# The order of the first transfers, and 1/rms behind the first products of the last FFN

## The chip, the cores and the metric

The kernel runs on one core of one Trainium2 chip. The metric is the device time of one execution in microseconds; the kernel before has a median of 1949.0 us in three runs (1946.32 to 1955.2). The engines are TensorE (PE, its weight loads are listed as PEld), VectorE (DVE), ScalarE (ACT), GpSimd (POOL) and SyncE (SP), which here issues the transfers.

## The reference

A backbone of two layers works on 256 latent and 256 context tokens of width 1024, all in fp32. Each layer has a SwiGLU FFN of width 2816, a mixer (eight attention heads, four gated DeltaNet heads, one output projection) and a second FFN. In front of each stands an RMS norm with a shift and a scale that come from a condition vector through `w_mod`:

```
y = xf * lax.rsqrt(jnp.mean(xf * xf, axis=-1, keepdims=True) + RMS_EPS)
h = modulate(rms_norm(x, gain), shift, scale)      # h * (1 + scale) + shift
gate, up = jnp.split(h @ w_in, 2, axis=-1)
x = x + 0.5 * gate_mod * ((jax.nn.silu(gate) * up) @ w_out)
```

The mods are `silu(c) @ w_mod[l] + b_mod[l]`, nine vectors of 1024 for the latent tokens and nine for the context. In the second layer the output projection and the last FFN are made for the latent tokens alone.

## The kernel before, in words

**Layout.** x lies transposed: eight tiles `x[d]` of 128 features by 512 tokens, the latent half in columns 0 to 255. A feature here means such a tile. fp32 operands are split in a high and a low part (`hh`, `hl` for the modulated x, `wh`, `wl` for weights: a cast on ACT, then a subtraction on DVE), and `mm3` makes each product as three matmuls: high by high, high by low, low by high. The times below count these matmuls as products.

**An FFN.** A unit is 128 columns of gate and 128 of up; it takes 8 features x 2 x 3 = 48 products and two PSUM tiles, each 512 tokens wide in the first three FFNs and 256 wide in the last (`ns == 1`). There are 22 units, in groups of 8, 8, 2 and 4; the out-product of a group follows a group later. The first two units of an FFN are begun as soon as the first half of the tokens is normed. In the very first FFN it is three units, taken feature by feature (L1111), with weights that come in half tiles (`weight_part`).

**A norm** has four steps: squares of x as soon as a feature is added up (`square_sum`), column sums of these on PE with a matrix of ones (`norm_stats`), the spread of 1/rms over the partitions, again on PE (`norm_spread`), and for each feature a product with gain, scale and 1/rms on DVE, the shift on ACT and the low part on DVE (`norm_apply`).

**The start.** The first two mods are made on PE from 32 transfers of `w_mod` (tiles `n`, 256 KB each), in products with 32 columns (`sc` is silu of c). The copies and transpositions behind them give `md`, and with it the features. Later mods are made on DVE, as sums of products over `w_mod` rows (tiles `junk`, 512 KB for two of them), laid in as filler.

**The order.** Nothing is issued in program order. `Build` records all work as nodes; `plan()` lays them out seven times with a list scheduler, for each engine, with the durations of `cost_of`, the delays of a table `LAT` between engines and a priority, and picks the order and the buffers; this is then written out engine by engine. In gaps of PE that the planner foresees to be longer than `WARM[1]` it puts matmuls on zeros (`zero`, L672), which nothing reads. All other instructions are written at one line of the emitter, L680 in the profile of before (L681 afterwards).

**Around the change.** `main` and `program` (L1864 to L1937) hold the start: the calls of `load` and `features` in L1907 to L1918, which the planner is free to move. `next_norm` makes the function `after` that starts the norm behind a residual addition; the last output projection calls it once for the latent half.

## Time and profile before

| | |
|---|---|
| median of three runs | 1949.0 us |
| profiled execution | 1952.2 us, span 1950.4 us |
| granted clock of TensorE, mean of the span | 0.991 |
| PE busy | 1901.5 us, 97% |
| DVE busy | 1366.0 us, 70% |
| ACT busy | 833.3 us, 43% |
| transfers | 280.96 MB, 144 GB/s in the mean |

The profiled execution is one of its own and stands 3.2 us above the median. PE is the engine that sets the time; its gaps and its clock are the places to look at. A row of the timeline gives the start, the busy time, engine, line, operation, what is written and read (buffer numbers left out), the count of like instructions in it, and in brackets how long the engine was idle before and what ended that.

### The profile page before, as it was taken

To read this page: it belongs to the slowest core of one execution; us is meant where nothing else is said; L and a number is where in the kernel's file an instruction comes from. 1 tells how busy PE (TensorE), PEld (TensorE's weight loads), DVE (VectorE), ACT (ScalarE), POOL (GpSimd) and SP (SyncE) were. 2 spreads that over 40 slices of the span, in tenths; PEclk is the share of its full clock that TensorE was granted. 3 is DMA by queue.
4 is the path that set the end of the run, shared out by engine and by line. 5 is a ranking of instruction groups with operands and counts; after the bars stand their busy time and mean duration, and the time that the engine had idled before them with its cause. 6 is when DMAs were issued, how large, how long until landed. Compare 5 with 4: busy or idle time off the path is not lost.

```text
span 1950.4 us, 29083 instructions
## 1 busy us (share of the span) xinstructions
PE 1901.5 (97%) x11145; PEld 1617.4 (83%) x11145; DVE 1366.0 (70%) x2776; ACT 833.3 (43%) x1612; POOL 26.9 (1%) x31
## 2 busy tenths in 40 slices
PE   8999999999999999999999999999999989899999
PEld 5888887787886879888888898888889877689999
DVE  5666677799987978666653586556337988986555
ACT  5322221258838455222222342221125974755433
POOL 1000000000001000000000000000000000000000
PEclk9999999999998999999999999999999999999999
DMA  9555555553324213555553245656334243136654
GB/s 329 179 153 160 162 177 175 170 169 117 112 81 117 98 44 95 165 162 179 166 162 102 72 146 179 201 177 203 110 98 147 88 114 109 44 114 201 184 182 122
DMA packets 104474, 280.96 MB, mean 144 GB/s; under 512 B 27024, under 2 KB 30480, under 8 KB 104336
## 3 DMA queue, kind: packets, MB, share of 16 engines
q1 hardware_dynamic: 104336, 279.12, 45.9%
q8 instruction: 87, 1.43, 0.3%
q14 instruction: 51, 0.42, 0.1%
HBM read 270.69 MB, written 8.39 MB: 143 GB/s over the span
## 4 chain that ended last, share of the span: by engine, by line
PE 76%; DVE 13%; ACT 4%; DMA 4%; issue 2%; SPq 0%; DVEq 0%; ACTq 0%
PE ps L680 76%; DVE d L680 3%; DVE n L680 2%; DMA wr<-w_mod 2%; DVE wl L680 2%; ACT d L680 1%; DVE wh L680 1%; ACT n L680 1%; DVE junk L680 1%; ACT wh L680 1%; DVE t L680 1%; DVE s L680 1%; DVE x L680 1%; ACT s L680 1%; ACT L680 1%
## 5 line engine op out<-in xcount | busy, mean ns | idle before, releaser
L680 PE MATMUL ps<-s,wh 128*128 128x512 f32 (+1 forms) x3344 | 912.9, 361 | 1.0 <-DVE s L680 0.5
L680 PEld LDWEIGHTS ps<-s,wh 128*128 128x128 f32 x3344 | 592.8, 189 | 100.3 <-issue 1.4
L680 PE MATMUL ps<-s,wl 128*128 128x512 f32 (+1 forms) x1672 | 603.5, 361 | 0.9 <-DVE wl L680 0.9
L680 ACT CAST wh<-wr 128x1024 fp32r<-128x1024 f32 (+2 forms) x341 | 350.4, 1037 | 479.1 <-PE ps L680 328.6
L680 DVE TENSOR_TENSOR wl<-wr,wh 128x1024 fp32r<-128x1024 f32 (+2 forms) x341 | 408.3, 1208 | 97.1 <-ACT wh L680 93.6
L680 DVE CUSTOM_DVE_ANT_0 junk<-wr,m,sm 128x1024 bf16<-128x1024 f32 x224 | 287.6, 1284 | 235.0 <-DMA wr<-w_mod 231.9
L680 PEld LDWEIGHTS ps<-s,wl 128*128 128x128 f32 x1672 | 314.8, 188 | 48.6 <-DVE wl L680 1.6
L680 PE MATMUL ps<-d,wh 128*128 128x256 f32 (+1 forms) x1344 | 300.4, 319 | 6.9 <-DVE x L680 3.9
L680 PEld LDWEIGHTS ps<-d,wh 128*128 128x128 f32 x1344 | 223.1, 191 | 30.3 <-issue 9.3
L680 PE MATMUL ps<-d,wl 128*128 128x256 f32 (+1 forms) x672 | 212.8, 317 | 1.2 <-DVE wl L680 1.2
L680 PE MATMUL ps<-n,wh 128*128 128x512 f32 (+1 forms) x640 | 178.3, 365 | 0.0
L680 DVE SCALAR_TENSOR_TENSOR x<-ps,hg,x 128x256 f32<-128x256 f32 x224 | 97.4, 478 | 93.2 <-PE ps L680 93.1
L680 ACT ACTIVATE d<-ps 128x512 f32<-128x512 f32 (+2 forms) x108 | 56.9, 529 | 237.1 <-PE ps L680 236.7
L680 PE MATMUL ps<-wh,s 128*128 128x512 f32 (+1 forms) x544 | 154.2, 360 | 0.3 <-DVE s L680 0.3
L680 PEld LDWEIGHTS ps<-d,wl 128*128 128x128 f32 x672 | 128.3, 191 | 9.5 <-DVE wl L680 1.7
L680 PEld LDWEIGHTS ps<-n,wh 128*128 128x128 f32 x640 | 115.4, 189 | 20.8
L680 PE MATMUL ps<-n,wl 128*128 128x512 f32 (+2 forms) x416 | 130.6, 347 | 0.7 <-DVE n L680 0.7
L680 DVE TENSOR_TENSOR d<-d,d 128x256 f32<-128x256 f32 (+29 forms) x310 | 111.6, 381 | 16.6 <-ACT d L680 12.0
L680 PEld LDWEIGHTS ps<-wh,s 128*128 128x128 f32 x544 | 96.4, 188 | 19.5 <-issue 5.2
L680 PE MATMUL ps<-wl,s 128*128 128x512 f32 (+1 forms) x272 | 96.6, 355 | 0.6 <-DVE wl L680 0.6
L680 DVE TENSOR_TENSOR d<-d,ps 128x512 f32<-128x512 f32 (+1 forms) x88 | 54.4, 618 | 58.4 <-PE ps L680 40.6
L680 PEld LDWEIGHTS ps<-n,wl 128*128 128x128 f32 x416 | 71.9, 189 | 10.7 <-issue 0.8
(163 smaller groups left out, 1563.7 us busy)
## 6 DMA issues: line engine op xcount, KB each, us to landing
wr<-w_in SPq DMA_DIRECT2D x171, 512.0 KB, 4.3
wr<-w_mod SPq DMA_DIRECT2D x128, 512.0 KB, 4.0
wr<-w_out SPq DMA_DIRECT2D x104, 512.0 KB, 4.2
wr<-wd SPq DMA_DIRECT2D x24, 512.0 KB, 3.8
n<-w_mod SPq DMA_DIRECT2D x32, 256.0 KB, 5.5
wr<-wg SPq DMA_DIRECT2D x8, 528.0 KB, 3.6
xd<-x SPq DMA_DIRECT2D x16, 256.0 KB, 4.5
x<-xd SPq DMA_DIRECT2D x16, 256.0 KB, 3.6
```

The source lines that it names most:

```text
L680: getattr(eng, name)(*[rv(x) for x in a], **{q: rv(x) for q, x in k.items()})
```

## The change

It has four parts.

1. The first transfers. While `nc.settled` is true, nodes of SP get a priority by their number, so SP issues them in program order. The program's order is changed with it: the mods of a feature come behind the weights' half tiles of that quarter or ahead of them, as the diff shows.
2. The planner's numbers: the delay behind a transfer, the bytes per microsecond, the thresholds for zero products, and a few durations. The whole order is made anew with them.
3. 64 columns of the constants that nothing reads are left out.
4. The last FFN. `norm_raw` writes, feature by feature, x times gain and scale in two parts without 1/rms, and the shift as two more columns; the first two units' products run on these 258 columns (`ffn_mm_raw`). `ffn_act_raw` multiplies gate and up by 1/rms (`self.rms`) and adds the shift's column when the sums are there. The other 20 units use the normed features as before.

```diff
+        n.settled = self.settled and eng == "sync"
...
-    "sync": {"tensor": 2.1, "vector": 2.1, "scalar": 2.1, "gpsimd": 2.1, "sync": 2.1},
+    "sync": {"tensor": 2.8, "vector": 2.8, "scalar": 2.8, "gpsimd": 2.8, "sync": 2.1},
...
-WARM = (0.8, 0.6, 0.7)
+WARM = (0.8, 0.3, 0.85)
...
+        self.prio = [n.i - 1e6 if n.settled else p for p, n in zip(self.prio, rec.nodes)]
...
-        return max(0.48, byts / 359e3) if eng == "sync" else 1.04
+        return max(0.48, byts / 330e3) if eng == "sync" else 1.04
...
+        if name == "tensor_tensor_reduce":
+            return 0.19 + n / 960
...
+    def norm_raw(self, lc, m, d):
...
+        nc, O, F32, a = self.nc, self.O, self.F32, self.na[:, d, 0:1]
+        x, c, e = self.x[d][:, :TL], slice(TL, T), slice(T, T + 2)
+        hh, hl, sh = self.hh[d], self.hl[d], lc["md"][:, 8 * m + d, 0:1].to_broadcast([128, 2])
+        nc.scalar.activation(hh[:, c], x, self.A.Copy, scale=a)
+        nc.vector.scalar_tensor_tensor(hl[:, c], x, a, hh[:, c].bitcast(F32), O.mult, O.subtract)
+        nc.vector.tensor_copy(hh[:, e], sh)
+        nc.vector.tensor_tensor(hl[:, e], sh, hh[:, e].bitcast(F32), O.subtract)
...
+            if raw:
+                self.rms = self.slot("rms")[:, :TL]
+                self.nc.scalar.copy(self.rms, bs[:, :TL])
...
+    def ffn_mm_raw(self, u):
+        w, p = u
+        for k in range(KD):
+            for i in range(2):
+                r = slice((k % 4 * 2 + i) * 128, (k % 4 * 2 + i + 1) * 128)
+                self.mm3(p[i][:, :TL + 2], (w[k // 4][0][:, r], w[k // 4][1][:, r]), (self.hh[k][:, TL:], self.hl[k][:, TL:]), k == 0, k == KD - 1)
+
+    def ffn_act_raw(self, u, tag):
...
+        nc.vector.tensor_tensor(g[:, c], pg[:, c], self.rms, O.mult)
+        nc.vector.tensor_copy(b[:, 0:1], pg[:, TL:TL + 1])
+        nc.scalar.activation(g[:, c], g[:, c], self.A.Silu, bias=b[:, 0:1])
+        nc.vector.tensor_tensor(t[:, c], pu[:, c], self.rms, O.mult)
+        nc.vector.tensor_copy(b[:, 1:2], pu[:, TL:TL + 1])
+        nc.vector.scalar_tensor_tensor(g[:, c], t[:, c], b[:, 1:2], g[:, c], O.add, O.mult)
...
                 with nc.urgent(100):
                     self.add_x(d, ps, gate, (s,))
                     self.square_sum(d, s)
+                    if after.raw:
+                        after.raw(d)
...
+        nc.settled = True
         self.cond()
...
-        load(0, 0)
         features(0, 0, 1)
-        load(0, 1, 2)
+        load(0, 0, 1, 2)
         features(0, 1, 1)
+        features(1, 0, 2)
         load(1, 0, 1, 2)
-        features(1, 0, 2)
+        features(2, 0, 2)
         for f in range(2):
             u[f].append(self.weight_begin())
         load(2, 0, 1)
-        features(2, 0, 2)
+        features(3, 0, 2)
         load(3, 0, 1)
-        features(3, 0, 2)
+        self.nc.settled = False
```

On PE at the start, these rows of before stand behind the last product of `w_mod`; `s` are features, `wh` and `wl` the halves of a unit's weights, `ps` its PSUM tiles:

```order
L680 MATMUL ps_485<-s_491,wh_449 128x512
L680 MATMUL ps_485<-s_506,wh_449 128x512
L680 MATMUL ps_485<-s_491,wl_475 128x512
L680 MATMUL ps_502<-s_491,wh_449 128x512
L680 MATMUL ps_502<-s_506,wh_449 128x512
L680 MATMUL ps_502<-s_491,wl_475 128x512
```

In the new order products of `w_mod` (32 columns, from tiles `n`) stand between the FFN's in this way from the first FFN product on:

```order
L681 MATMUL ps_397<-s_442,wh_303 128x512
L681 MATMUL ps_397<-s_449,wh_303 128x512
L681 MATMUL ps_397<-s_442,wl_379 128x512
L681 MATMUL ps_411<-n_424,sc_79 32x128 x4
L681 MATMUL ps_418<-s_442,wh_303 128x512
L681 MATMUL ps_418<-s_449,wh_303 128x512
L681 MATMUL ps_418<-s_442,wl_379 128x512
L681 MATMUL ps_411<-n_438,sc_79 32x128 x4
```

Before has 18 FFN products ahead of the last product of `w_mod`, the new order has 75.

On PE at the last norm, before has zero products around the column sums of the squares (`con` by `d`) and the spread of 1/rms (`d` by `con`):

```order
L672 LDWEIGHTS zero_83
L672 MATMUL ps_15895<-zero_83 128x256
L680 MATMUL ps_15918<-con_188,d_15792 128x1 x2
L672 LDWEIGHTS zero_83
L672 MATMUL ps_15921<-zero_83 128x256
```

Now the products on the raw x follow the last ones of the output projection (`d` by `wh`) at once:

```order
L681 MATMUL ps_15950<-s_15556,wh_15802 128x258
L681 MATMUL ps_15950<-s_15564,wh_15802 128x258
L681 MATMUL ps_15950<-s_15556,wl_15832 128x258
L681 MATMUL ps_15926<-d_15699,wh_15775 128x256
L681 MATMUL ps_15926<-d_15717,wh_15775 128x256
L681 MATMUL ps_15926<-d_15699,wl_15797 128x256
L681 MATMUL ps_15962<-s_15556,wh_15802 128x258
L681 MATMUL ps_15962<-s_15564,wh_15802 128x258
L681 MATMUL ps_15962<-s_15556,wl_15832 128x258
L681 MATMUL ps_15950<-s_15580,wh_15802 128x258
```

The column sums stand 24 products behind the last one of the projection, and there are no zero products any more. Three raw products have moved ahead of it.

On DVE at the norm behind the first FFN of layer 0, before has a reduction over a tile of `w_mod` (`junk`) just ahead of the last unit's product of gate and up and the additions to x:

```order
L680 TENSOR_TENSOR wl_2874<-wr_2773,wh_2869 128x1024
L680 TENSOR_TENSOR d_2898<-d_2898,ps_2832 128x512
L680 ISA junk_803,md_400<-wr_2887,m_638,sm_370 128x1024
L680 ISA md_400 128x1
L680 TENSOR_TENSOR d_2920<-d_2898,d_2912 128x512
L680 TENSOR_TENSOR wl_2922<-wr_2807,wh_2905 128x1024
L680 SCALAR_TENSOR_TENSOR x_79<-ps_2900,hg_1226,x_79 128x256
```

Now both reductions of such a tile stand ahead of the product of gate and up:

```order
L681 TENSOR_TENSOR wl_2882<-wr_2783,wh_2877 128x1024
L681 ISA junk_910,md_326<-wr_2866,m_724,sm_85 128x1024
L681 ISA md_326 128x1
L681 ISA junk_910,md_326<-wr_2866,m_761,sm_85 128x1024
L681 ISA md_326 128x1
L681 TENSOR_TENSOR d_2906<-d_2906,ps_2841 128x512
L681 TENSOR_TENSOR wl_2923<-wr_2817,wh_2915 128x1024
L681 TENSOR_TENSOR d_2931<-d_2906,d_2921 128x512
L681 SCALAR_TENSOR_TENSOR x_170<-ps_2908,hg_1316,x_170 128x256
```

One more reduction has moved ahead of the additions to x.

## Rows read from the trace of the kernel before

**Rows 1.** Page, busy us of an engine, its share of the span.
```profile
PE 1901.5 (97%) x11145; PEld 1617.4 (83%) x11145; DVE 1366.0 (70%) x2776; ACT 833.3 (43%) x1612; POOL 26.9 (1%) x31
```
**Rows 2.** Windows, FFN products of the start: us, busy (count), clock, DMA share, GB/s.
```profile
0.00:50.00 50.00, 17.45 (x65) 0.93 0.96 330
0.00:100.00 100.00, 67.45 (x281) 0.97 0.74 249
```
**Rows 3.** Timeline of PE at the start.
```profile
28.80 0.80 PE L680 MATMUL ps<-s,wh 128*128 128x512 f32 x1
...
30.48 0.73 PE L680 MATMUL ps<-s,wh 128*128 128x512 f32 x2
...
31.74 0.74 PE L680 MATMUL ps<-s,wh 128*128 128x512 f32 x2
...
34.11 1.30 PE L680 MATMUL ps<-n,sc 128*32 128x128 f32 x40
...
38.69 0.42 PE L680 MATMUL ps<-n,sc 128*32 128x128 f32 x8
```
**Rows 4.** Timeline of PE at the last norm.
```profile
1750.61 0.28 PE L680 MATMUL ps<-d,wl 128*128 128x256 f32 x1
1750.73 1.38 PE L672 MATMUL ps<-zero 128*128 128x256 bf16 x11
1752.46 0.61 PE L680 MATMUL ps<-con,d 128*128 128x1 f32 x4 [0.36 <-DVE d L680]
...
1754.19 0.70 PE L680 MATMUL ps<-d,con 128*128 128x256 f32 x2 [0.23 <-DVE d L680]
...
1756.64 0.39 PE L680 MATMUL ps<-s,wh 128*128 128x256 f32 x1 [0.26 <-DVE s L680]
```
**Rows 5.** Timeline of PE at the norm behind the first FFN.
```profile
385.30 0.77 PE L680 MATMUL ps<-d,wh 128*128 128x256 f32 x2 [3.86 <-DVE x L680]
...
404.04 0.61 PE L680 MATMUL ps<-con,d 128*128 128x1 f32 x4 [4.05 <-DVE d L680]
```
**Rows 6.** Windows of PE, PEld, DVE, ACT, POOL; then clock, DMA share, GB/s.
```profile
25.00:30.00 5.00, 4.42 (x42) 2.37 (x42) 4.33 (x14) 2.54 (x6) 0.00 (x0) 0.66 0.99 342
385.00:390.00 5.00, 4.70 (x29) 4.73 (x30) 5.00 (x12) 0.00 (x0) 0.00 (x0) 0.69 0.44 129
600.00:650.00 50.00, 46.28 (x383) 36.04 (x381) 35.67 (x98) 36.56 (x113) 6.44 (x5) 0.90 0.41 133
1550.00:1600.00 50.00, 44.40 (x221) 36.53 (x222) 45.66 (x132) 39.90 (x102) 3.53 (x2) 0.93 0.28 80
```
**Rows 7.** Chain of waits, its last link: start, us, what.
```profile
1760.53 186.06 PE ps L680 x1556
```
**Rows 8.** Timeline of ACT and DVE at the start.
```profile
12.83 1.28 ACT L680 ACT_TABLE_LOAD   x1
...
16.64 0.37 ACT L680 COPY d<-ps 128x256 f32<-128x256 f32 x1 [0.25 <-PE ps L680]
...
23.51 1.23 DVE L680 SCALAR_TENSOR_TENSOR d<-x,na,d 128x256 f32<-128x256 f32 x3
...
24.66 0.88 DVE L680 SCALAR_TENSOR_TENSOR s<-d,md,s 128x256 fp32r<-128x256 f32 x2
...
26.21 0.62 ACT L680 CAST wh<-wr 128x512 fp32r<-128x512 f32 x1 [0.91 <-DMA wr<-w_in]
```
**Rows 9.** DMA issues: count, KB each, median us to landing.
```profile
n<-w_mod SPq DMA_DIRECT2D x32, 256.0 KB, 5.5
```
**Rows 10.** Timeline of ACT and DVE at the last norm.
```profile
1749.71 0.40 ACT L680 ACTIVATE d<-x 128x256 f32<-128x256 f32 x1
...
1754.92 1.26 DVE L680 SCALAR_TENSOR_TENSOR d<-x,na,ps 128x256 f32<-128x256 f32 x3 [0.79 <-PE ps L680]
```
**Rows 11.** Timeline of DVE at the norm behind the first FFN.
```profile
380.94 1.28 DVE L680 CUSTOM_DVE_ANT_0 junk<-wr,m,sm 128x1024 bf16<-128x1024 f32 x1 [3.96 <-DMA wr<-w_mod]
...
383.89 3.22 DVE L680 SCALAR_TENSOR_TENSOR x<-ps,hg,x 128x256 f32<-128x256 f32 x8
```

## The prediction
> **What bounds the kernel now.** I read the page's busy shares first. TensorE is busy 1901.5 us [rows 1] of a span of 1950.4, so only about 49 us can be won by closing its gaps, and everything else only by taking products away or by a higher granted clock. The change takes away no product of the reference. So I looked for gaps of PE, in the windows of the whole span and then in the PE timeline, in each place that the change touches. There are four kinds. The start: the first FFN product stands at 28.80, and 65 products are done at 50 us [rows 2, 3]. The last norm: between the last output-projection product and the stream of the last FFN [rows 4]. The norm behind the first FFN, where PE waits twice [rows 5]. And stalls inside the mixers [rows 6]. The last link of the chain of waits is 186 us of PE without a break [rows 7]: behind 1760.53 nothing can be won but by an earlier start of it, and every microsecond closed ahead of it is a microsecond of the end.

> **Part 1, the first transfers in program order.** Before, nearly all first modulation products come ahead of the FFN: 18 FFN products (six groups of three) stand before the last of them at 38.69 [rows 3]. Afterwards 75 do, in 25 groups of three, and between them stand 24 sets of four w_mod products (the trace counts 8 for such a set). Two numbers make the term: when the first group starts, and what a period costs.

> The start. Feature 0 now needs only four w_mod tiles, and the half tiles of the weights are requested behind them. So the scale by 1/rms sets it. Its copies end at 17.0 before (16.64 + 0.37 [rows 8]). ACT has three weight casts of 0.62 around these copies, but one pair of table loads of 1.28 fewer ahead [rows 8]; I take 17.4. From the first scaled feature to its low part the rows run from 23.51 to 24.66 + 0.44 (half of the two in that row), 1.6 us [rows 8]; the modulation's small sums ahead of it I estimate at 0.6. So the first product starts at 17.4 + 0.6 + 1.6 = 19.6, 9.2 earlier than 28.80.

> The period. In the one stretch of before in which the two kinds alternate at full speed, a group starts at 30.48 and the next at 31.74: 1.26 us [rows 3]. In a stream three FFN products cost 0.69, since 216 (281 - 65) take 50 us, 0.2315 each [rows 2]; and 40 w_mod products in a row take 1.30, 0.26 for 8 of them [rows 3]. So 0.31 of each period is the price of alternating. Before pays it 6 times, after 24 times.

> [...]

> The sum: the 75th FFN product ends at 19.6 + 24 x 1.26 + 0.69 = 50.5. Before it ends at 50.0 + 10 x 0.2315 = 52.3 [rows 2]. Start: **-1.8**. What hides the rest: transfers. Up to the last w_mod tile SP requests some 12.9 MB; at 330 GB/s [rows 2] that is 39 us, and with the 5.5 from issue to landing [rows 9] at most 45, ahead of its turn on PE at about 49. The last two features are first read 33 products, 7.6 us, behind the last w_mod product, and features 2 and 3 five groups, some 5 us, behind theirs; the chain between is the 2.2 us of above for one feature, and with a second feature, the copy and the transposition I put it at 4. Bounds of the term: -5 if two pairs of table loads' worth and the casts come out of the start; +4 if the cover of 5 us is short by 2 at each of the three places where features change.

> **Part 4, 1/rms behind the products.** Before, the last out-projection product starts at 1750.61 with the zeros behind it from 1750.73; 28 of the 1584 products of the last FFN stand before the unbroken link of 1556 at 1760.53 [rows 4, 7]. At 186.06 / 1556 = 0.1196 us each these 28 are 3.35 us, so the gap is 9.80 - 3.35 = 6.45 us. It holds zero products, the column sums, the spread of 1/rms and the wait for the first three scaled features. Afterwards the first units' 96 products need only x times the gain and scale, per feature, as soon as that feature is added up; three of them already stand ahead of the last projection product, and the column sum of the squares stands 24 products behind it. Each feature costs ACT one pass of 0.40, DVE one of 0.42 (1.26 / 3 [rows 10]) and two short ones, on engines that have 96 x 0.12 = 11.5 us for the last two features. The sums and the spread stay and now stand in the stream: 0.61 and 0.70 by their rows, 1.3 [rows 4]. The two columns more per product are 2 / 256 of 11.5, 0.1. The applying behind costs DVE two multiplications, two copies and one fused operation for each unit; 20 more units follow on PE, so I put nothing. Last FFN: -6.45 + 1.3 + 0.1 = **-5.0**; bounds -6.4 (sum and spread hide too) and -2 (the first features or the PSUM of two waiting units make PE wait for 3 us).

> **Part 2, the planner's numbers.** All orders are made anew; most pieces differ by a few swaps, and I read only the norm behind the first FFN. There DVE waits 3.96 us for a tile of w_mod at 380.94, and only behind it multiplies gate and up for the last unit of the group and adds to x from 383.89 [rows 11]; PE stands 3.86 us until 385.30 and runs until 388 at the lower of its levels: the window 385 to 390 has a granted clock of 0.69, some 1.5 us lost [rows 5, 6]. A second wait of 4.05 at 404.04 is for the sum of squares, behind the same reductions on DVE. In the new order that tile's two reductions stand earlier, with a product, a weight subtraction and a product behind them before x. Had DVE nothing to wait for there, 3.9 + 1.5 would go; but one reduction more (1.28) comes ahead of the last sum of squares, so the second wait grows: -4.1. I take half, **-2.1**, since whether the tile has landed hangs on requests that the order does not time. Bounds: -8 (both waits go) and +1 (the first stays, the second grows). The other stretches I put at 0, with -6 and +6: the two mixers lose 3.7 and 5.6 us of PE in the windows from 600 and 1550 [rows 6], and a swap there can give or take a few.

> **Part 3,** the constant without 64 columns, is 32 KB of DMA, behind the start: nothing.

> **Sum.** -1.8 - 5.0 - 2.1 = -8.9. The profiled execution took 1952.2 us (span 1950.4 and 1.8 around it), so 1943.3 on its scale; it stands 3.2 above the median of the three runs, 1949.0, and so the forecast is **1940 us**.

> **The rivals.**
> (a) Alternation at the lower clock: slower. Before's first alternating group from 28.80 to 30.48 took 1.68 instead of 1.26 [rows 3]; PE had been waiting for transfers, and the window 25 to 30 has a granted clock of 0.66 [rows 6]. If the many short waits keep PE at the lower of its two levels for the whole first stretch, the 75th product ends at 19.6 + 24 x 1.68 + 1.0 (the last three) = 60.9, +8.6. With -5.0 of the last FFN and nothing from the new order this gives 1955.8, **1952.6** against the median. It decides from a period of 1.54 on, where 5.0 are eaten. For it: 1.68 was measured; against it: the clock in before rose within that very stretch, with products of 512 columns running. [...]
> [...]
> (c) The new order also mends the mixers, 10 of the 16 us that they lose in idle and clock in the windows of [rows 6]: **1930**.
> (d) The new order takes back: the wait at 385 stays (+2.1) and the mixers lose 4: **1946**.
> (e) The raw path does not do what it says: the first two units' PSUM tiles and the low parts come late, so PE stands 3 to 4 us at the same place: **1944**.

> **How the numbers follow.** Forecast 0.40, with its own range 1935 to 1945; (a) 0.12, (b) 0.08, (c) 0.16, (d) 0.18, (e) 0.06. A measurement of this kernel can tell about 0.5%, 9.7 us: faster means below 1939.3, slower above 1958.7. Faster: all of (b) and (c), 0.24, and a bit under half of the forecast, 0.18: 0.42. Slower: a third of (a), where the mixers lose 6 more, and a tail of (d): 0.07. The same: 0.51. Range: 1930 reaches (c), 1952 nearly all of (a); what is left out is below 1930 half of (c) and above 1952 half of (a), with small tails.

> **What would show it.** First FFN product near 19.6 and 65 such products before 48; groups of about 1.26 apart; if they are 1.7 apart and the window 20 to 50 has a clock below 0.8, (a) holds. At the last norm no zero products and no PE wait over 0.5 us between projection and FFN, and the link to the end longer than 190 us. At the first norm PE waits of 8 us together before, about 5 after. Wrong altogether would be a time below 1930 or above 1952, or a right one by other places than these.

## The result and the profile after

The changed kernel takes 1921.97 us (median of 4 runs, 1920.52 to 1924.05), the kernel before 1951.16 in the same comparison: ratio 0.9852, 95% interval [0.9826, 0.9879]. That is 29 us, three times the forecast 9, and outside its range.

Page of the changed kernel, busy time by engine:

```profile
PE 1895.0 (99%) x11121; PEld 1601.1 (83%) x11121; DVE 1374.2 (71%) x2808; ACT 833.1 (43%) x1619; POOL 26.5 (1%) x31
```

The span is 1922.0 instead of 1950.4, with a mean granted clock of 0.996 instead of 0.991. PE is idle for 27.0 us instead of 48.9, and busy for 6.5 us less [rows 1].

**The start.** Windows of the FFN products, which answer to [rows 2], and the timeline of PE, to [rows 3]:

```profile
0.00:50.00 50.00, 22.85 (x72) 1.00 0.88 305
0.00:100.00 100.00, 72.34 (x285) 1.00 0.72 244
```

```profile
20.69 0.74 PE L681 MATMUL ps<-s,wh 128*128 128x512 f32 x2
...
23.30 0.73 PE L681 MATMUL ps<-s,wh 128*128 128x512 f32 x2
...
24.55 0.73 PE L681 MATMUL ps<-s,wh 128*128 128x512 f32 x2
...
51.10 0.43 PE L681 MATMUL ps<-n,sc 128*32 128x128 f32 x8
```

The first product stands at 20.69 and groups of three follow at 1.25 us, at a granted clock of 1.00. The last w_mod product stands at 51.10 with 75 FFN products ahead of it. By 100 us there are 285 products instead of 281: 4 x 0.23 = 0.9 us won.

**The norm behind the first FFN.** The timeline of PE has one wait left there [rows 5], of 0.71 us where 3.86 and 4.05 stood, and the window from 385 shows a granted clock of 1.00 instead of 0.69 [rows 6]. The other two windows lie in the mixers; they hold other work than before, since everything comes earlier now, and the mixers are read by stage below.

```profile
393.14 0.61 PE L681 MATMUL ps<-con,d 128*128 128x1 f32 x4 [0.71 <-DVE d L681]
```

```profile
385.00:390.00 5.00, 5.00 (x44) 5.00 (x43) 4.69 (x14) 2.16 (x5) 0.00 (x0) 1.00 0.20 45
...
600.00:650.00 50.00, 46.16 (x429) 41.78 (x430) 41.76 (x141) 31.29 (x89) 0.00 (x0) 0.92 0.34 109
1550.00:1600.00 50.00, 46.71 (x218) 37.82 (x218) 45.08 (x120) 33.83 (x68) 3.40 (x2) 1.00 0.48 138
```

In the window from 385 PE executes 44 products instead of 29. The column sums stand at 393.14 instead of 404.04: 10.9 us earlier, of which 0.9 are the start's.

**The last norm.** Timeline of PE [rows 4], then the last link of the chain of waits [rows 7]:

```profile
1729.64 0.28 PE L681 MATMUL ps<-d,wl 128*128 128x256 f32 x1
1729.76 0.40 PE L681 MATMUL ps<-s,wh 128*128 128x258 f32 x2
...
1732.51 0.28 PE L681 MATMUL ps<-s,wl 128*128 128x258 f32 x1
1732.84 0.60 PE L681 MATMUL ps<-con,d 128*128 128x1 f32 x4
1733.31 0.49 PE L681 MATMUL ps<-s,wh 128*128 128x258 f32 x2
...
1735.79 0.28 PE L681 MATMUL ps<-s,wl 128*128 128x258 f32 x1
1735.91 0.59 PE L681 MATMUL ps<-d,con 128*128 128x256 f32 x2
1736.15 0.59 PE L681 MATMUL ps<-s,wh 128*128 128x258 f32 x2
```

```profile
1732.84 185.29 PE ps L681 x1560
```

There are neither zero products nor waits. The link of 185.29 us begins at the column sums, 24 products behind the projection. From the last product of the projection to the last of all it is 188.56 us (1918.20 - 1729.64) instead of 196.04 (1946.65 - 1750.61): 7.5 us won.

**All of it by stage**, from products that stand at the same place in both kernels (the first column sums of each norm, the last product of the projection, the last product):

| to | before | after | won in the stage |
|---|---|---|---|
| column sums behind the first FFN | 404.04 | 393.14 | 10.9 |
| column sums ahead of the second FFN | 745.77 | 726.27 | 8.6 |
| the second half's sums ahead of the second mixer | 1502.76 | 1486.02 | -2.8 |
| last product of the output projection | 1750.61 | 1729.64 | 4.2 |
| last product | 1946.65 | 1918.20 | 7.5 |

So the stretches with the mixers gained where I had put zero, and the two FFNs between them lost 2.8 us, although PE is busy in them throughout.

One more line answers for the rest. Waits of DVE, in the kernel before and then in the changed one (sum, times, longest):

```profile
DVE junk L680 <- DMA wr<-w_mod: 231.9, 102, 5.2
```

```profile
DVE junk L681 <- DMA wr<-w_mod: 99.9, 57, 4.7
```

The reader is to see that the sum has more than halved. It is no loss by itself, since DVE is not the bound (busy 71% against 99% of PE), but what stands behind such a wait on DVE comes late, and PE may need it; e9 shows below what that can cost.

### The profile page after: what moved, and what is told of

Same layout as the page of the kernel before. It is cut to its first block, busy times and chain, and to the rows that moved or that the text cites. A ratio compares the mean times of both kernels' runs of the same rounds, so it can differ in the third digit from the quotient of the medians.

```text
span 1922.0 us, 29078 instructions
## 1 busy us (share of the span) xinstructions
PE 1895.0 (99%) x11121; PEld 1601.1 (83%) x11121; DVE 1374.2 (71%) x2808; ACT 833.1 (43%) x1619; POOL 26.5 (1%) x31
## 4 chain that ended last, share of the span: by engine, by line
PE 83%; DVE 9%; ACT 5%; issue 1%; DMA 1%; SPq 0%; DVEq 0%; ACTq 0%
PE ps L681 83%; DVE n L681 2%; ACT n L681 2%; DVE wh L681 1%; ACT d L681 1%; DVE d L681 1%; DVE wl L681 1%; ACT wh L681 1%; DVE s L681 1%; DMA n<-w_mod 1%; DVE mx L681 1%; ACT L681 1%; ACT s L681 1%; DVE t L681 0%; DVE x L681 0%
## 5 line engine op out<-in xcount | busy, mean ns | idle before, releaser
L681 PE MATMUL ps<-s,wh 128*128 128x512 f32 (+2 forms) x3344 | 912.9, 361 | 0.0
L681 PEld LDWEIGHTS ps<-s,wh 128*128 128x128 f32 x3344 | 586.3, 188 | 102.5 <-issue 4.8
L681 PE MATMUL ps<-s,wl 128*128 128x512 f32 (+2 forms) x1672 | 599.6, 359 | 0.0
L681 DVE TENSOR_TENSOR d<-d,d 128x256 f32<-128x256 f32 (+28 forms) x310 | 111.4, 379 | 11.8 <-ACT d L681 7.3
```

What stands on the lines that cost most here:

```text
L681: getattr(eng, name)(*[rv(x) for x in a], **{q: rv(x) for q, x in k.items()})
```

## The experiments

**The parts, each alone.** e1 is the kernel before with part 2 only, e2 with part 4 (and 3), e3 with part 1, e4 the changed kernel without part 4, e8 without part 1. The core of each edit:

```diff
# e4, and the tiles s 512 wide again
-            elif i == 0 and len(halves) == 1:
+            elif False:
-            after.raw = raw if ns == 1 else None
+            after.raw = None
# e8: load and features as before, and
-        nc.settled = True
```

> Only part 2 (the planner's numbers) is put into the kernel before. Theory (the numbers carry the gain: DVE is no longer ordered behind tiles of w_mod that have not landed, so the waits of PE at the first norm, 3.86 and 4.05 us, and stalls in the first mixer go): 14 to 20 us faster than before, 1931 to 1937 us, and DVE waits for w_mod near 100 us in place of 232. Rival (the gain comes from the settled order of the first transfers and the raw path, or from a lucky order): within 6 us of before, 1945 to 1957 us.

> Only part 4 (1/rms behind the products in the last FFN; the constants without 64 columns too) is put into the kernel before. Theory: 5 to 8 us faster, 1943 to 1946 us, since the gap of 6.45 us at the last norm goes and 1.3 us of sums come into the stream; the waits of the first norm stay. Rival (the remade order alone moves much): any time more than 6 us away from 1944.

> Only part 1 (the first transfers in program order, with the planner's old numbers). Theory: 0 to 2 us faster, 1949 to 1951 us, from the start alone. Rival (a settled start is what puts the transfers of later stages right): over 8 us faster, under 1943 us.

> The changed kernel without part 4. Its order on PE is that of the changed kernel up to the second layer's mixer. Theory: 6 to 9 us slower than the changed kernel, 1928 to 1931 us, of which 5 at the last norm. Rival (the raw path's gain is hidden or given back by the mixer's order): 1922 to 1925 us.

> The changed kernel without part 1 (the planner places the first transfers itself). Theory: 4 to 7 us slower than the changed kernel, 1926 to 1929 us, all of it within the first 60 us, as with the planner's numbers alone, where the hundredth FFN product stands at 60.4. Rival (part 1 is worth nothing beside the rest): 1921 to 1924 us.

| | median us | ratio to before | DVE waits for w_mod |
|---|---|---|---|
| e1 part 2 | 1936.37 | 0.9928 [0.9913, 0.9943] | 96.9 |
| e2 part 4 | 1946.46 | 0.9992 [0.9980, 1.0004] | 203.3 |
| e3 part 1 | 1946.14 | 0.9980 [0.9968, 0.9992] | 211.2 |
| e4 without part 4 | 1930.32 | 0.9898 [0.9883, 0.9913] | 98.3 |
| e8 without part 1 | 1929.30 | 0.9887 [0.9872, 0.9901] | 97.1 |

Part 2 is the greatest part: e1's time lies within the theory's 1931 to 1937 us, its gain of 13.5 us just below the 14 to 20. e3 is faster by more than the start itself and less than its rival said. e2 gave less than expected: its last stage is 188.6 us, 7.4 better, and its first sums come 3.9 us earlier, but the remade order loses 2.1 us from there to the second FFN (343.9 instead of 341.7) and 2.2 in the FFNs (759.2 instead of 757.0). The traced executions are 7.3 us apart, the medians only 3.4, and the interval holds 1. On the changed kernel the raw path is worth 8.4 us (e4), as the theory had it, and part 1 7.3 (e8), a little above its 4 to 7; e8's trace shows 4.4 us of it by the hundredth product. But part 1 is worth so much there because of part 2: with the planner's new numbers its own start has the hundredth FFN product at 61.5 us (e8), with the settled one at 57.1, and before at 58.0.

**Which number of the planner.** e5 has only the delay and the rate of transfers, e6 only WARM, e7 only the durations; e13 the delay alone, e14 the rate alone; e9 and e10 move the first two the other way and twice as far.

```diff
-    "sync": {"tensor": 2.1, "vector": 2.1, "scalar": 2.1, "gpsimd": 2.1, "sync": 2.1},
+    "sync": {"tensor": 2.8, "vector": 2.8, "scalar": 2.8, "gpsimd": 2.8, "sync": 2.1},   # e5, e13; e9 1.4, e10 3.5
-        return max(0.48, byts / 359e3) if eng == "sync" else 1.04
+        return max(0.48, byts / 330e3) if eng == "sync" else 1.04   # e5, e14; e9 388e3, e10 301e3
```

> Of the planner's numbers only the two for transfers (delay 2.8 in place of 2.1, 330e3 bytes per us in place of 359e3) are put into the kernel before. Theory (transfers were planned to land too early, which puts reductions over w_mod tiles that have not landed ahead of urgent work on DVE): 8 to 15 us faster than before, 1935 to 1942 us, DVE waits for w_mod about 100 us, first column sums by 398 us. Rival (the durations of DVE and ACT carry it): within 3 us of before, DVE waits over 180 us.

> Of the planner's numbers only WARM (zero products in gaps from 0.3 us on) is put into the kernel before. Theory: the granted clock is lost for less time (34 us at half clock before), 2 to 5 us faster, 1945 to 1948 us, waits of DVE as before. Rival (the clock's losses are only a consequence of waits and the zero products come in the wrong places): within 2 us of before.

> Of the planner's numbers only the durations (0.12 us more for each reduction, short or narrow instructions of DVE dearer, 0.1 more for 32 partitions on ACT) are put into the kernel before. Theory (transfers carry the gain): within 3 us of before, 1947 to 1953 us, DVE waits for w_mod over 180 us. Rival: 5 to 12 us faster, above all in the mixers, whose narrow instructions were planned too short.

> The kernel before with the planner's two numbers for transfers moved the other way by as much (delay 1.4, 388e3 bytes per us). Theory (the numbers act through the waits of DVE for tiles that have not landed): waits for w_mod above 260 us, and 3 to 15 us slower than before, 1954 to 1966 us. Rival (any remade order is a draw, and that of before was a bad one): waits as they fall, a time from 1930 to 1950 us.

> The same two numbers moved twice as far as in the change (delay 3.5, 301e3 bytes per us). Theory: the waits of DVE for w_mod fall further, below 90 us, but PE no longer waits for them, so the time stays within 4 us of 1930. Rival (a draw): anywhere from 1930 to 1950 us.

> Of the two numbers for transfers only the delay (2.8 in place of 2.1) is put into the kernel before. Theory (the moment at which a tile may be read is what was planned too early): 1928 to 1935 us, DVE waits for w_mod 100 to 140 us. Rival (the rate, since requests are spaced too closely and queue up): within 5 us of before, waits over 180 us.

> Of the two numbers for transfers only the rate (330e3 in place of 359e3 bytes per us) is put into the kernel before. Theory (the delay carries it): 2 to 8 us faster than before, 1942 to 1948 us, waits 170 to 220 us. Rival (the rate carries it): 1928 to 1935 us, waits below 140 us.

A tile of w_mod is 512 KB. The planner's time from its request to its reading is the delay plus bytes by rate; the page's issue list has a median of 4.0 us for it before and 4.2 after.

| | planned us | DVE waits for w_mod | median us | ratio to before |
|---|---|---|---|---|
| e9 | 1.4 + 1.35 = 2.75 | 271.2 | 2012.11 | 1.0317 [1.0286, 1.0347] |
| before | 2.1 + 1.46 = 3.56 | 231.9 | 1951.16 | |
| e14 rate | 2.1 + 1.59 = 3.69 | 161.7 | 1934.77 | 0.9911 [0.9884, 0.9938] |
| e13 delay | 2.8 + 1.46 = 4.26 | 118.0 | 1933.51 | 0.9909 [0.9881, 0.9937] |
| e5 both | 2.8 + 1.59 = 4.39 | 103.3 | 1930.33 | 0.9895 [0.9877, 0.9912] |
| e10 | 3.5 + 1.74 = 5.24 | 41.0 | 1940.86 | 0.9953 [0.9936, 0.9970] |

The waits follow the planned time without exception, and from e9 to e5 the time falls with them, by 82 us. The mechanism is the theory's: planned too early, a reduction is put ahead of urgent work on DVE and holds it until its tile lands. In e9, the waits of PE and of DVE around 320 us:

```profile
324.16 0.79 PE L680 MATMUL ps<-d,wl 128*128 128x512 f32 x1 [6.13 <-DVE wl L680]
```

```profile
319.56 1.28 DVE L680 CUSTOM_DVE_ANT_0 junk<-wr,m,sm 128x1024 bf16<-128x1024 f32 x1 [3.83 <-DMA wr<-w_mod]
...
320.89 1.28 DVE L680 CUSTOM_DVE_ANT_0 junk<-wr,m,sm 128x1024 bf16<-128x1024 f32 x1
...
322.88 2.35 DVE L680 TENSOR_TENSOR wl<-wr,wh 128x1024 fp32r<-128x1024 f32 x2
```

DVE waits 3.83 us for the tile, and the low part of a weight behind it comes late for PE by 6.13. All waits of PE for such low parts, in the kernel before and then in e9 (sum, times, longest):

```profile
PE ps L680 <- DVE wl L680: 2.8, 3, 1.2
```

```profile
PE ps L680 <- DVE wl L680: 40.4, 11, 8.3
```

The sizes were missed. I expected e9 3 to 15 us slower, and it is 62: in its trace 29 of them stand ahead of the first sums (433.23) and 36 in the FFNs (792.9 instead of 757.0), and the mean granted clock is 0.974 instead of 0.991. e5 was expected to win 8 to 15 us and won 20.8. For e14 the theory had 1942 to 1948; it has the time of its rival, with more waits than that allowed (161.7, not below 140). And e10 fell out of its bound of 4 us around 1930: its waits are the smallest of all, but the time is 10 us above e5. In its trace the hundredth FFN product is at 59.6 instead of 55.1, and the FFNs between the mixers take 760.6 us instead of 756.6; the second of these goes with the distance between products that is explained below. So the sum of waits tells where to look and not the time: e10 has the least waits and not the best time. That the rate alone (e14), which cuts the waits by only a third, gains nearly as much as both agrees with dear places that the first small step frees, those at the norm behind the first FFN (its sums stand at 391.1 to 391.4 in e5, e13 and e14). That any remade order would do is contradicted by e2, e3 and e6, remade with the old numbers for transfers and durations: 1946.46, 1946.14 and 1952.74 us. But how much of one order's gain is chance, these runs do not separate.

WARM alone does nothing (e6: 1952.74, ratio 1.0008 [0.9998, 1.0018]), against the 2 to 5 us expected. The durations alone (e7) give 1933.31, ratio 0.9908 [0.9891, 0.9924], where the theory said within 3 us and its rival 5 to 12: it is 17.8 us faster than before, beyond both. The waits fell too, to 161.3 us; a likely reason is that DVE planned slower leaves more time for a tile as well. Parts of part 2 thus seem to do much the same thing, and their gains do not add: 20.8 (e5) and 17.8 us (e7) alone, 13.5 all together (e1). Beside e5, e1 loses at the start (the hundredth product at 60.4 instead of 55.1) and in the FFNs (760.8 instead of 756.6 us).

**Fewer of the numbers on the changed kernel.** e11 takes WARM back, e12 also the durations; e16 is e5 with the raw path and the planner's own start.

> The changed kernel with the old thresholds for zero products. Theory (they bring nothing, and alone changed the time by 1.6 us at most): 1919 to 1924 us. Rival (zero products in gaps from 0.3 us on keep the clock up): 3 to 6 us slower than the changed kernel, with more than 25 us at the lower clock.

> The changed kernel with the old thresholds and the old durations, so that of part 2 only the two numbers for transfers remain. Theory (those alone gave more than all of part 2, 1930 against 1936): 3 to 8 us faster than the changed kernel, 1914 to 1919 us: 1930 less 7.5 at the last norm and some 4 at the start. Rival (gains of remade orders do not add): 1920 to 1926 us.

> The kernel before with the two numbers for transfers and the raw path, without the settled first transfers. Theory (the last norm's gain adds to that of the transfers' numbers, and the planner's own start was 2 us better there than the settled one): 1921 to 1925 us. Rival (gains of remade orders do not add): 1926 to 1932 us.

They give 1923.36 (0.9859 [0.9832, 0.9887]), 1928.56 (0.9885 [0.9856, 0.9915]) and 1929.75 (0.9887 [0.9861, 0.9914]). e11 is as expected. e12 is 6.6 us above the changed kernel, beyond its theory and its rival. e16 lies where its rival had it: its last stage is 188.7 us, 6.0 better than in e5, but the median is only 0.6 lower. Its trace gives back 1.5 us from the first sums to the second FFN, 3.4 in the FFNs (760.1 instead of 756.6) and 0.7 in the last mixer. The raw path makes the tiles `s` 514 columns wide, and what that does to the FFNs comes next.

**The FFNs in which PE never waits.** The mean distance from one 512-column product to the next, taken from the trace between 1170 and 1440 us, is 0.2308 us before, 0.2319 after, 0.2305 in e5, 0.2322 in e1 and 0.2321 in e10; that of the 256-column products of the last FFN 0.1191 before and 0.1185 after. e15 changes only the width of the tiles `s`, and leaves out the 64 unused columns to make room; the order on every engine is that of before:

```diff
-        return self.sp.tile([128, 512], dtype or self.F32, ..., bufs=self.BUFS[tag])
+        return self.sp.tile([128, 514 if tag == "s" else 512], dtype or self.F32, ..., bufs=self.BUFS[tag])[:, :512]
```

> The kernel before with the tiles s 514 wide in place of 512 (and the unused constants dropped to make room); the order on PE, DVE and ACT is that of before. Theory (where operands lie in the on-chip memory sets the spacing of products): 512-column products in a steady stretch 0.2318 us apart in place of 0.2307, and 256-column ones 0.1185 in place of 0.1191, as in the changed kernel; in all within 4 us of before. Rival (the order sets the spacing): 0.2307 and 0.1191 as before.

It took 1951.54 us (1.0002 [0.9990, 1.0015]), with distances of 0.2318 and 0.1185: those of the changed kernel, in the order of before. So the place of the operands sets the distance. Sorted by the address of the moving tile less that of the weights, as the program places them, modulo 256 bytes, the distances of before between 830 and 1070 us are 0.2289 us at 0 (613 products) and 0.2337 at 128 (426). A weight buffer is 1056 x 4 = 4224 bytes, 16 x 256 + 128, so every second one lies 128 off. e17 (e5 with other places and without the 64 unused columns) and e18 (the changed kernel with other places, `s` 512 wide again) put `wr` buffers and four pads of 128 bytes between the ten that PE reads, so that nine lie at 0:

```diff
+PLACES = [("wh", 0), ("wr", 0), ("wl", 0), ("wr", 1), ("wh", 1), ("wr", 2), ("wl", 1), ("wr", 3), ("wh", 2), None, ("wl", 2), None, ...]
# e18, too
-        x, c, e = self.x[d][:, :TL], slice(TL, T), slice(T, T + 2)
+        x, c, e = self.x[d][:, :TL], slice(TL, T), slice(TL - 2, TL)
```

> The kernel of e5 (before with the planner's two numbers for transfers; the unused constants dropped) with the same order of all engines' work, but the 14 weight buffers placed so that 9 of the 10 that PE reads start a whole number of 256 bytes away from the tiles of features and activations (in e5 half of them are 128 off). Theory (where the two operands lie against each other sets the spacing of products; in the traces a distance of 128 modulo 256 goes with 0.2333 us, 0 with 0.227 to 0.230): FFN products of 512 columns 0.2285 to 0.2295 us apart in place of 0.2304, and 5 to 9 us faster than e5, 1921 to 1925 us. Rival (the distance only goes along with something of the order, as which product follows which): 0.2304 and 1930 us as in e5.

> The changed kernel with the tiles s 512 wide again (the two shift columns stand in columns 254 and 255, over the normed part that is written only later) and the weight buffers placed as in e17; the order on PE and SP is that of the changed kernel. Theory: 512-column products 0.2285 to 0.2295 us apart in place of 0.2319, some 4750 of them in the three wide FFNs, 11 to 16 us faster than the changed kernel, 1906 to 1911 us, with up to 1 us given back in the last FFN. Rival (spacing does not follow the places, or PE then waits for weights): 1918 to 1924 us.

e17: 1913.31 us, ratio 0.9815 [0.9799, 0.9831]; e18: 1904.74 us, ratio 0.9776 [0.9758, 0.9793]. Against the kernels with the same order on PE, e5 and the changed one, the medians are 17 us lower (15 by the ratios to before); 5 to 9 and 11 to 16 were expected. The gain stands where the products of 512 columns are: of 14.3 us between the spans of e5 and e17, 6.2 are won up to the first sums and 8.0 in the two FFNs between the mixers. Windows of PE (busy, count, clock, DMA share, GB/s) of one FFN stretch, in before, e15, e5, e17, e18 and the changed kernel:

```profile
1200.00:1300.00 100.00, 100.00 (x435) 1.00 0.64 199
```

```profile
1200.00:1300.00 100.00, 100.00 (x433) 1.00 0.65 196
```

```profile
1200.00:1300.00 100.00, 100.00 (x436) 1.00 0.62 187
```

```profile
1200.00:1300.00 100.00, 100.00 (x441) 1.00 0.63 192
```

```profile
1200.00:1300.00 100.00, 100.00 (x441) 1.00 0.60 190
```

```profile
1200.00:1300.00 100.00, 100.00 (x433) 1.00 0.61 184
```

The count is what to read: all six are busy for 100 us at the full clock, and one executes 433 products where another executes 441. In e18 the distance is 0.2276; between 830 and 1070 us its products at 0 stand 0.2271 apart (969), the rest at 128 0.2342 (72). The last FFN gives some back: 190.5 us instead of 188.6, with 0.1197 between its 256-column products. e18 is the best version found, and beats both kernels.

## Why the prediction was wrong

- **Part 1**, -1.8: the mechanism was right, with 0.9 won by 100 us. The first product came at 20.69 instead of 19.6; the period of 1.25 was as worked out, at a granted clock of 1.00, so rival (a) fell. The chance of 0.08 for (b), a part of the 0.24 for faster, stood for a price of alternating that vanishes, a period of 0.95 us (1.26 - 0.31); no run shows such a period, and the shortest in the changed kernel's trace is 1.14. The last w_mod product came at 51.1, about 2 us later than the 49 of the prediction. The price of alternating stayed: wherever w_mod products stand between two groups, the next group starts 1.14 to 1.37 us behind, and 0.8 where none do. What makes this price, the runs don't show.
- **Part 4**, -5.0: right in mechanism, 7.5 in size. The sums and the spread cost 0.68 (1732.51 + 0.12 to 1733.31) and 0.24 (1735.91 to 1736.15) of the stream and not 1.3, since their busy times overlap with the neighbours'; three products had moved ahead of the projection's last (0.36); and closer 256-column products gave 0.9, as e15 shows by itself (195.1 instead of 196.0 us). Another 0.5 stood in before just behind 1760.53, where five products follow at 0.19 to 0.26 us instead of 0.12, which the link counts as unbroken work; some 0.3 stays without a cause. The link to the end was forecast as longer than 190 us; it is 185.29, since it begins at the column sums.
- **Part 2**, -2.1 and "the other stretches I put at 0": this is the step that failed. Behind the start, up to the first sums, 10.0 us were won where I took half of 4.1, and the mixers, taken as 0 with 6 either way, gave 8.6 and 4.2. I read the order at one place and asked which wait would move. What should have been read is the sum of DVE's waits for `w_mod`, 231.9 us, beside the planned 3.56 us and the page's 4.0 to landing: a planner that is early by 0.4 us in the median can put reductions too early anywhere. With the two numbers for transfers alone (e5) the first sums stand at 391.14, 12.9 us earlier than before, and the stretch to the second FFN takes 334.8 us instead of 341.7. e9, e13, e14 and e5 show that waits and time answer to this number, and e10 that the time does so only up to a point. Rival (c) had the mixers, at a chance of 0.16: 10 us there, of 16 that are nearer 18 by its rows, and 12.8 were measured; the 10 us ahead of the first sums it had not.
- **The clock.** Of the 28.4 us of span, about 10 are the clock, an estimate from the mean granted clocks: (1 - 0.991) x 1950 = 17.6 us of full-speed work lost before, (1 - 0.996) x 1922 = 7.7 after. They are part of the gains by stage above and do not come on top. I had priced one of these stretches (1.5 us at 385); in before's trace the 256-column products stand 0.213 us apart in it, at 0.50 up to 388.1, and 0.118 behind it, at 1.00.
- The two FFNs' loss of 2.8 us was in no term. e15, with before's order and the wider tiles, shows most of it: there the stretch takes 759.4 us, 2.4 more than before.

What stays open: which single reorderings in the mixers carry their 8.6 and 4.2 us, and why e12 is slower than the changed kernel.

## What to carry to other kernels

Where a planner fixes the order, compare its assumed durations with the trace's, transfers first: the issue list has the time to landing (here 4.0 us, with 3.56 planned), and a large sum of waits on an engine that is not the bound (here DVE's 231.9 us for `w_mod`) says that its work is queued behind data that has not come. Such a sum is a sign and not a price. Try such a number in both directions before pricing single places, and expect that gains of remade orders do not add (here 20.8 and 17.8 us alone, 13.5 together). Where PE is busy throughout, count products per 100 us: if two kernels with the same products differ there, as 433 and 441 did here, look at where the operands lie.
